# Block products by sevens in the second MLP's up projection, with sums of weights prepared in the first MLP

## The chip, the cores and the metric

The kernel runs on one core of a Trainium2 chip. TensorE multiplies (PE in the profile; PEld is its loading of weights), VectorE (DVE), ScalarE (ACT) and GpSimd (POOL) do everything elementwise, and DMA queues, issued mostly from SyncE (SP), move data between DRAM and the chip's memory. The metric is the device time of one execution in microseconds.

## The reference

One inference step of a two-layer decoder trunk, with 512 prompt tokens and 8 sample tokens (520 columns in all) and a model width of 1024. The part that matters here is the MLP of each layer, which both groups of tokens pass through with the same weights:

```python
def sq_relu_mlp(h, g, w_up, w_down):
    a = jax.nn.relu(rmsnorm(h, g) @ w_up)
    return (a * a) @ w_down
hp = hp + sq_relu_mlp(hp, norm_ffn[l], mlp_up[l], mlp_down[l])
hs = hs + sq_relu_mlp(hs, norm_ffn[l], mlp_up[l], mlp_down[l])
```

The up weights are 1024 x 4096 and the down weights 4096 x 1024, in float32. Ahead of the first MLP is a pooling mixer, between the two MLPs lies the attention of the second layer (with a compressed, a selected and a window branch), and a final RMSNorm follows the second MLP.

## The kernel before

Tokens lie along the free dimension (520 columns, handled as two halves of `NH` = 260), features along the 128 partitions. Every float32 product is made from three products of a rounded type: a weight tile is split into a high part (ACT copies it into the rounded type, L221) and a low part (DVE subtracts, `lo_of`, L201), the data likewise, and high x high, high x low and low x high are added up in PSUM (`gemm`, L237). A weight tile is 128 x 8 x 128, 512 KB. A unit is 8 blocks x 3 products x 2 column halves = 48 matmuls of 260 columns.

Each MLP goes through four quarters of its 4096 hidden features. A quarter has 8 up units, one for each 128 hidden features, and then 8 down units, which add the quarter's contribution to the residual `h`. After an up unit `up_post` applies relu, the norm's factor `rn` and the square, and splits the result into a tile `at` (a ring of eight). In the second MLP the down units of the last quarter are cut into column halves (`last_quarter`), so that the final norm of the first half can run early; they start with `at` tile 0 and come to the last tile at the end.

The order of work is written by `run`. It goes through a list of jobs. Each job has a `pe` part (matmuls), a `prep` (the split of its weights), a `post` list (what follows the matmuls: entry d is written d + 1 jobs later) and loads. These two lines set the order:

```python
due = ahead - sum(k > i for k in with_prep[:done])      # after job i: keep two splits ahead
late.setdefault(i + 1 + d, []).insert(0, f)             # entry d of job i's post, ahead of older ones
```

All `late` entries of a job are written before its matmuls, its splits after them. An engine runs its instructions in the order in which they were written. Weight loads go through SP into a ring of three buffers (`wraw`); a load waits until the low part of the split three tiles earlier has read its buffer. The split parts of a weight tile lie in rings of two (`whi`, `wlo`), and a split waits until the matmuls that use the older tile in its place are done. Products lie in PSUM in a ring of two `mm` tiles of two banks each, and `aux` tiles of one bank.

In the first MLP the list also holds fillers, small products for the compressed branch of the sample group. The tuple `FILLERS` says after which of the 64 units one filler comes; some fillers bring a tiny companion job ahead of them:

```python
FILLERS = (0, 1, 1, 1, 0, 1, 1, 0, 0, 1, 1, 1, 1, 0, 1, 1, 0, 1, 1, 0, 0, 1, 0, 1, 0, 1, 0, 1, 0, 1, 1, 1, 0, 0, 0, 1, 1, 0, 1, 1, 0, 1, 0, 0, 0, 1, 0, 0, 1, 1, 0, 1, 0, 1, 0, 1, 0, 1, 0, 0, 0, 1, 1, 1)
```

A filler splits its own data on ACT and DVE (L473 to L477). POOL is idle in the first MLP. In the second MLP there are no fillers. The pool `wz` holds the split weights of the whole last quarter.

Of the kernel before, what the change touches and what calls it, by code (L numbers as in the profile page):

```python
# [151 lines left out]
def trunk(tc, a, o):  # L152
# [23 lines left out]
    hsave = pool("hd", space=bass.MemoryType.DRAM).tile([P, CT, NT], F32, name="hsave")  # L176
# [23 lines left out]
    def lo_of(out, x, hi):  # L200
        V.tensor_tensor(out, x, hi.bitcast(F32), op=OP.subtract)  # L201
# [127 lines left out]
    def norm_job(emit=lambda: None):  # L329
        box = {}  # L330

        def pe():
            for i in range(2):
                box[i] = st["aux"]()
                TE.matmul(box[i][:, 0:NH], onesm, accn[:, i * NH:(i + 1) * NH], start=True, stop=True)  # L335

        def post():
            inv_rms(box)
            emit()

        return Job(pe=pe, post=post)
# [353 lines left out]
    def mlp_jobs(l, filler, done, before=lambda: None):  # L695
        ap, kind = {}, "w2" if l else "w"

        def open_a():
            ap["p"] = pool("ap")
            if l:  # L700
                pool("wz")
# [21 lines left out]
        js = []  # L723
        for q in range(4):
            for f in range(8):
                js.append(gemm_job(W(a["up"][l, 8 * q + f]), xpairs, up_post(8 * q + f), kind=kind))
                if not l and q in (1, 2):
                    js[-1].after = lambda x=("wink", "winv")[q - 1], b=f: S.dma_start(o[x][b], a_in[x][b])
                if q == f == 0:
                    js[-1].post.insert(0, None)  # L730
                    js[-1].after = lambda: (before(), open_a())
                    js.append(norm_job())
                js += filler()
            for ct in range(CT):
                xs = (lambda q=q: [(at[8 * q + k][:, 0], at[8 * q + k][:, 1]) for k in range(8)])
                if l and q == 3:
                    continue
                js.append(gemm_job(W(a["down"][l, q, ct]), xs, down_post(q, ct), kind=kind))
                js += filler()
        if l:  # L740
            js += last_quarter(xs)
        js.append(Job(hook=lambda: close(*["wz"] * l, "ap")))
        return js

    def last_quarter(xs):


        ws = [W(a["down"][1, 3, ct], home=lambda: (pools["wz"][1], CT)) for ct in range(CT)]
# [24 lines left out]
        def norm(i):  # L773
            sl = slice(i * NH, (i + 1) * NH)
            box = {}

            def pe():
                box["ps"] = st["aux"]()
                TE.matmul(box["ps"][:, 0:NH], onesm, accn[:, sl], start=True, stop=False)  # L779
                TE.matmul(box["ps"][:, 0:NH], onesm, sq[i][:, sl], start=False, stop=True)  # L780

            def post():
                S.activation(rn[:, sl], box["ps"][:, 0:NH], AF.Ln, bias=eps[:, 0:1])  # L783
                S.activation(rn[:, sl], rn[:, sl], AF.Exp, scale=-0.5)  # L784

            def rows(c):
                for ct in (c, c + 1):
                    if i and ct in ahead:
                        G.tensor_tensor(h[:, ct, sl], h[:, ct, sl], rn[:, sl], op=OP.mult)  # L789
                        continue  # L790
                    V.scalar_tensor_tensor(h[:, ct, sl], h[:, ct, sl], gv[:, 5, ct:ct + 1], rn[:, sl], op0=OP.mult, op1=OP.mult)  # L791
                (S if i and c in (2, 6) else nc.sync).dma_start(o["y"][:, c:c + 2, sl], h[:, c:c + 2, sl])
            steps = [lambda c=c: rows(c) for c in range(0, CT, 2)]
            return Job(pe=pe, post=[lambda: (post(), [f() for f in steps])] if i else [post] + steps)

        for i in range(2):
            js += [unit(ct, i) for ct in range(CT)]
        js.insert(CT + 1, norm(0))
        return js + [norm(1)]
# [1151 lines left out]
```

## Time and profile before

| | us |
|---|---|
| median of 3 runs | 1389.52 |
| lowest and highest run | 1387.92, 1392.79 |
| the profiled execution, its time | 1392.16 |
| the profiled execution, its span | 1390.0 |
| TensorE busy in the span | 1345.2 |
| DVE, ACT, POOL busy | 836.7, 570.8, 190.3 |

All further times are those of the one profiled execution, counted from the start of its span. A line of the profile names a line of the kernel (L237), and where a helper writes the instruction, the helper's line. A matmul's own duration is longer than the distance to the next one, because matmuls are pipelined; for the pace, one divides a stretch by its matmuls. The granted clock (PEclk) is TensorE's, as a share of full speed.

### The profile page before, as it was taken

Reading aid. Unit: us, or ns where it says so; the run is one execution under the profiler, and the core shown is the slowest. Engines: PE = TensorE matmul, PEld = TensorE weight load, DVE = VectorE, ACT = ScalarE, POOL = GpSimd, SP = SyncE. Lnnn points to the kernel's source line nnn. Section 1 sums busy time; section 2 is a strip of 40 time slices with the busy share of each in tenths; the row PEclk is TensorE's granted clock in tenths of the full one; section 3 lists DMA queues with packets and bytes.
Section 4 is the critical chain, followed back from the end, with each engine's and each line's share of the span. In section 5 each row is a group of like instructions: output and inputs, shape, how many; then the busy total and the mean of one; then the engine's idle time right before and its main releaser. Section 6 shows DMA issues by size and latency. Waiting matters only on the chain. (4 is left out here: it accounts for less than half of the span.)

```text
span 1390.0 us, 27557 instructions
## 1 busy us (share of the span) xinstructions
PE 1345.2 (97%) x10827; PEld 1261.3 (91%) x10827; DVE 836.7 (60%) x1307; ACT 570.8 (41%) x1012; POOL 190.3 (14%) x265
## 2 busy tenths in 40 slices
PE   7999999999999999999998999998999999999997
PEld 6788999999999999989996777667999999999996
DVE  2788766565565476556878887554554353453563
ACT  3655443333333243464445677563432222221231
POOL 0000000000000000012455764751000000000000
PEclk9999999999999999999999999999999999999999
DMA  7755244554455232339505675766223233322321
GB/s 261 224 153 185 77 136 137 167 165 139 139 172 161 76 107 77 98 131 231 142 26 177 187 207 185 215 204 193 92 87 94 91 94 95 96 92 91 92 91 62
DMA packets 110554, 189.52 MB, mean 136 GB/s; under 512 B 13641, under 2 KB 81482, under 8 KB 109786
## 3 DMA queue, kind: packets, MB, share of 16 engines
q1 hardware_dynamic: 102202, 166.65, 38.6%
q0 software_dynamic: 7168, 12.21, 3.6%
q10 hardware_dynamic: 1056, 8.92, 1.9%
q8 instruction: 85, 1.39, 0.4%
q14 instruction: 43, 0.35, 0.1%
HBM read 177.59 MB, written 16.43 MB: 140 GB/s over the span
## 5 line engine op out<-in xcount | busy, mean ns | idle before, releaser
L237 PE MATMUL mm<-xn,whi 128*128 128x260 f32 (+1 forms) x2784 | 450.0, 284 | 0.4 <-DVE xn L201 0.3
L237 PEld LDWEIGHTS mm<-xn,whi 128*128 128x128 f32 (+1 forms) x2784 | 383.1, 189 | 1.6 <-DVE xn L201 0.5
L201 DVE TENSOR_TENSOR wlo<-wraw,whi 128x1024 fp32r<-128x1024 f32 x163 | 200.6, 1231 | 257.5 <-ACT whi L221 257.2
L237 PE MATMUL mm<-at,whi 128*128 128x260 f32 x2048 | 332.6, 281 | 0.3 <-DVE at L201 0.3
L221 ACT ACTIVATE whi<-wraw 128x1024 fp32r<-128x1024 f32 x163 | 171.5, 1053 | 313.6 <-PE mm L237 257.1
L237 PEld LDWEIGHTS mm<-at,whi 128*128 128x128 f32 x2048 | 283.9, 188 | 1.0 <-DVE at L201 0.5
L237 PE MATMUL mm<-xn,wlo 128*128 128x260 f32 (+1 forms) x1392 | 281.1, 283 | 0.0
L237 PE MATMUL mm<-at,wlo 128*128 128x260 f32 x1024 | 215.9, 282 | 0.0
L237 PEld LDWEIGHTS mm<-xn,wlo 128*128 128x128 f32 (+1 forms) x1392 | 215.2, 188 | 0.0
L237 PEld LDWEIGHTS mm<-at,wlo 128*128 128x128 f32 x1024 | 161.4, 188 | 0.0
L201 DVE TENSOR_TENSOR clo<-craw,chi 128x512 fp32r<-128x512 f32 x128 | 85.3, 686 | 43.6 <-ACT chi L439 28.6
L710 ACT ACTIVATE at<-tmp 128x520 fp32r<-128x520 f32 x64 | 40.9, 639 | 143.2 <-DVE tmp L708 143.2
L1144 POOL TENSOR_TENSOR P<-P,sm 128x1024 f32<-128x1024 f32 (+1 forms) x64 | 81.9, 1290 | 3.8
L711 DVE TENSOR_TENSOR tmp<-tmp 128x520 f32<-128x520 f32 x64 | 44.8, 701 | 45.1 <-ACT at L710 45.1
L1129 ACT ACTIVATE P<-sc,sm 128x512 f32<-128x512 f32 (+3 forms) x128 | 66.0, 529 | 8.4 <-DVE sm L1117 8.2
L818 POOL MEMSET V2c<- 128x1024 f32 x1 | 1.0, 957 | 473.0 <-PE mm L237 473.0
L1244 PE MATMUL pt<-cst,P 128*128 128x128 f32 x320 | 53.0, 282 | 10.5 <-POOL P L1144 5.5
L789 POOL TENSOR_TENSOR h<-h,rn 128x260 f32<-128x260 f32 x2 | 1.9, 946 | 439.7 <-ACT rn L784 439.7
L1244 PEld LDWEIGHTS pt<-cst,P 128*128 128x128 f32 x320 | 37.3, 142 | 26.0 <-issue 6.8
L708 DVE SCALAR_TENSOR_TENSOR tmp<-mm,rn 128x520 f32<-128x520 f32 x64 | 44.5, 695 | 26.1 <-PE mm L237 21.6
L1117 DVE TENSOR_REDUCE sm<-sc 128x2 f32<-128x1024 f32 (+1 forms) x64 | 50.7, 815 | 13.2 <-PE sc L1090 8.8
L439 ACT ACTIVATE chi<-craw 128x512 fp32r<-128x512 f32 x64 | 37.0, 623 | 51.0 <-PE hid L451 35.4
(291 smaller groups left out, 1982.0 us busy)
## 6 DMA issues: line engine op xcount, KB each, us to landing
craw<-in_cc_dram SPq DMA_DIRECT2D x256, 128.0 KB
wraw<-in_up_dram SPq DMA_DIRECT2D x64, 512.0 KB
wraw<-in_down_dram SPq DMA_DIRECT2D x64, 512.0 KB
wraw<-in_selv_dram SPq DMA_DIRECT2D x62, 128.0 KB
wraw<-in_selk_dram SPq DMA_DIRECT2D x59, 128.0 KB
kvs<-in_selk_dram SPq DMA_DIRECT2D x53, 128.0 KB
kvs<-in_selv_dram SPq DMA_DIRECT2D x50, 128.0 KB
wraw<-in_wkv_dram SPq DMA_DIRECT2D x12, 512.0 KB
```

Source lines behind the costliest of these rows:

```text
L201: V.tensor_tensor(out, x, hi.bitcast(F32), op=OP.subtract)
L221: S.activation(hi, raw, AF.Copy)
L237: TE.matmul(ps[0:m, i, 0:NH], wt[:, koff + k, 0:m], x[:, i * NH:(i + 1) * NH], start=(k == 0 and wt is w.hi and x is xh), stop=(k == n - 1 ...
L439: S.activation(hv, src, AF.Copy)
L708: V.scalar_tensor_tensor(halves(r), view(ps), 0.0, halves(rn), op0=OP.max, op1=OP.mult)
L710: S.activation(t[:, 0], r, AF.Square)
L711: V.tensor_mul(r, r, r)
L789: G.tensor_tensor(h[:, ct, sl], h[:, ct, sl], rn[:, sl], op=OP.mult)
L1117: V.tensor_reduce(sm[:, c:c + 2], src, axis=AX.XY if len(src.shape) == 4 else AX.X, op=OP.max, negate=True)
L1129: S.activation(dst, src[:, b], AF.Exp, bias=sm[:, c:c + 1], accum_out=sm[:, m + c:m + c + 1])
L1144: G.tensor_tensor(x, x, sm[:, c:c + 2, None].to_broadcast(list(x.shape)), op=OP.mult)
L1244: TE.transpose(ps[:, 128 * x:128 * x + 128], ab["P", t, s, q][:, c:c + 128], ident)
```

## The change

In quarters 1 to 3 of the second MLP two up units become one pair, and the pair is calculated by Strassen's scheme (in its form with fifteen additions). The 256 x 1024 block of weights and the 1024 x 520 block of data are cut in two in both directions, so that a pair is a product of 2 x 2 blocks; a block of weights is 4 tiles of 128 x 128, a block of data 4 x 128 rows by 260 columns. Seven block products (12 matmuls of 260 columns each) take the place of eight.

- The data's seven left operands `X` are made once, during quarter 0: `normed` scales each tile by norm and weight while the up units run, and `moving` makes the sums and splits them while the down units run. So in these quarters `rn` is already in the data.
- Four of the weights' sums are made during the first MLP: 48 steps (`sum_steps`), each for a quarter of one pair's blocks, load 256 KB by two POOL DMAs, make four additions of 128 x 128 on DVE and store 256 KB by a POOL DMA in `sums` in DRAM. Each buffer exists once. Step n is spread over the `post` of units: a unit's extra entry makes the additions and the store of one step and issues the load of the next.
- A pair loads S13 and S24 (two sums each), A1 (the first tile's weights as they are) and A22 (half a tile). Their split parts go to a ring of four places: the two of `whi` and `wlo`, and two in the memory of `h`'s old tile (`dead`); A22 has its own.
- The seven products run as jobs pe5, pe1, pe6, pe2, pe7, pe3, pe4; the first four carry the splits of S13, A1, S24 and A22, the fifth an empty one. Sums of products are put together on DVE (`common`, `c22`, `c12`, `c21`), relu and squares run on ACT (two squares of each tile), the low part on DVE (`low`). `c22` reads the PSUM bank to which pe4 then adds.
- `open_x` opens the memory for `X` where `wz` was; `wz` is opened after the last pair, with six tiles, and the last quarter's first two weight tiles go to the ring of two.

```diff
-            for f in range(8):
+            if l and q:
+                js += [j for i in range(4) for j in seven_jobs(q, i, at, ap)]
+            for f in range(8 if not (l and q) else 0):
                 js.append(gemm_job(W(a["up"][l, 8 * q + f]), xpairs, up_post(8 * q + f), kind=kind))
...
+        else:
+            steps = [sum_steps(n) for n in range(48)]
+            for j, old, new in zip(units[4:], [()] + steps, [x[:1] for x in steps] + [()]):
+                j.post.append(lambda fs=(*old[1:], *new[:1]): [f() for f in fs])
...
+    def sum_steps(n):
+        pair, j = divmod(n, 4)
+        box = {}
+        def load():
+            box["w"] = pools["pf"][1].tile([P, 2, 2, 128], F32, name="sraw", bufs=1)
+            src = a["up"][1, 8 + 2 * pair:10 + 2 * pair].rearrange("f p (h j) n -> p f h j n", h=2)[:, :, :, j]
+            for f in range(2):
+                G.dma_start(box["w"][:, f], src[:, f])
+        def add():
+            w, x = box["w"], pools["pf"][1].tile([P, 4, 128], F32, name="sout", bufs=1)
+            box["x"] = x
+            V.tensor_tensor(x[:, 0], w[:, 1, 0], w[:, 1, 1], op=OP.add)
+            V.tensor_tensor(x[:, 1], w[:, 0, 0], w[:, 1, 0], op=OP.subtract)
+            V.tensor_tensor(x[:, 2], x[:, 0], w[:, 0, 0], op=OP.subtract)
+            V.tensor_tensor(x[:, 3], w[:, 0, 1], x[:, 2], op=OP.subtract)
+        def store():
+            G.dma_start(sums[pair].rearrange("p (s j) n -> p s j n", j=4)[:, :, j], box["x"])
+        return load, add, store
...
+    def moving(i):
+        x = sv["xt"].rearrange("p (k c) (h n) -> p k h c n", k=2, h=2)
+        B = [[x[:, k, i] for i in range(2)] for k in range(2)]
+        if i == 3:
+            V.tensor_tensor(B[0][0], B[0][1], B[0][0], op=OP.subtract)
...
+        S.activation(sv["X"][:, i, 0], src, AF.Copy)
+        lo_of(sv["X"][:, i, 1], src, sv["X"][:, i, 0])
+    def ring():
+        n = sv["n"]
+        sv["n"] += 1
+        if n % 4 < 2:
+            return [wp.tile([P, 8, 128], F32R, name=x, bufs=2) for x in ("whi", "wlo")]
+        if n == 2:
+            sv["dead"] = con.tile([P, 4, 2, NT], F32R, name="h").rearrange("p t z n -> p t (z n)")
+        return [sv["dead"][:, 2 * (n % 4 - 2) + i, 0:1024].rearrange("p (k n) -> p k n", n=128) for i in range(2)]
+    def seven_jobs(q, i, at, ap):
...
+        S13, A1, S24, A22 = D(s_[:, 0]), D(a["up"][1, f]), D(s_[:, 1]), D(a["up"][1, f + 1][:, 4:8], 4)
+        def times(w, k0, x, out, first=True, last=True):
+            for k in range(4):
+                for wt, part in ((w.hi, 0), (w.hi, 1), (w.lo, 0)):
+                    TE.matmul(out, wt[:, k0 + k], sv["X"][:, x, part, k], start=(first and k == 0 and wt is w.hi and part == 0),
+                              stop=(last and k == 3 and wt is w.lo), skip_group_check=True)
+        def pe7():
+            times(S13, 4, 4, box["e"])
+        def pe4():
+            times(A22, 0, 6, box["e"], first=False)
+        def keep1():
+            box["p1"] = small("p1")
+            S.activation(box["p1"], box["a"], AF.Copy)
+        def common():
+            box["u2"], box["u4"] = small("u2"), small("u4")
+            V.tensor_tensor(box["u2"], box["b"], box["p1"], op=OP.add)
+            V.tensor_tensor(box["u4"], box["c"], box["u2"], op=OP.add)
+        def c22():
+            V.tensor_tensor(box["r"][1][:, NH:], box["e"], box["u4"], op=OP.add)
+        def c12():
+            r = box["r"][0]
+            V.tensor_tensor(r[:, NH:], box["d"], box["u4"], op=OP.add)
+            S.activation(r[:, NH:], r[:, NH:], AF.Relu)
+            squares(0)
+        def c21():
+            r = box["r"][1]
+            V.tensor_tensor(r[:, 0:NH], box["e"], box["u2"], op=OP.add)
+            S.activation(r, r, AF.Relu)
+            squares(1)
...
+        return [job(pe5, S13), job(pe1, A1, keep1), job(pe6, S24, common), job(pe2, A22, c11), nothing(job(pe7, None, c22)),
+                job(pe3, None, c12, lambda: low(0)), job(pe4, None, *((c21, lambda: low(1)) if i < 3 else (lambda: (c21(), low(1)),)))]
```

## Rows read from the trace of the kernel before

**Rows 1.** The page: span, and busy time with share and instructions of TensorE.

```profile
span 1390.0 us, 27557 instructions
...
PE 1345.2 (97%) x10827; PEld 1261.3 (91%) x10827; DVE 836.7 (60%) x1307; ACT 570.8 (41%) x1012; POOL 190.3 (14%) x265
...
```

**Rows 2.** Timeline of the SP queue, two quarters of the second MLP.

```profile
...
1081.32 40.53 SPq L210 DMA_DIRECT2D wraw<-in_up_dram  x8
1127.28 40.49 SPq L210 DMA_DIRECT2D wraw<-in_down_dram  x8
...
```

**Rows 3.** Timeline of ACT: a weight split, second MLP.

```profile
...
1027.28 1.06 ACT L221 ACTIVATE whi<-wraw 128x1024 fp32r<-128x1024 f32 x1 [2.16 <-PE mm L237]
...
```

**Rows 4.** Timeline of DVE around that split.

```profile
...
1028.37 1.23 DVE L201 TENSOR_TENSOR wlo<-wraw,whi 128x1024 fp32r<-128x1024 f32 x1 [1.79 <-ACT whi L221]
1029.51 0.69 DVE L708 SCALAR_TENSOR_TENSOR tmp<-mm,rn 128x520 f32<-128x520 f32 x1
...
```

**Rows 5.** Waits from 1000 us on: us in total, times, longest.

```profile
...
ACT whi L221 <- PE mm L237: 173.4, 53, 4.7
...
```

**Rows 6.** Groups by form, from 960 us on: busy us, mean ns, idle before.

```profile
...
L201 DVE TENSOR_TENSOR wlo<-wraw,whi 128x1024 fp32r<-128x1024 f32 x71 | 87.0, 1225 | 170.3 <-ACT whi L221 170.3
...
L221 ACT ACTIVATE whi<-wraw 128x1024 fp32r<-128x1024 f32 x70 | 74.1, 1059 | 194.3 <-PE mm L237 183.4 <-issue 10.9
L711 DVE TENSOR_TENSOR tmp<-tmp 128x520 f32<-128x520 f32 x32 | 22.4, 700 | 22.6 <-ACT at L710 22.6
...
L710 ACT ACTIVATE at<-tmp 128x520 fp32r<-128x520 f32 x32 | 20.5, 639 | 62.2 <-DVE tmp L708 62.2
...
L760 DVE TENSOR_TENSOR h<-h,mm 128x260 f32<-128x260 f32 x16 | 6.8, 422 | 13.5 <-PE mm L237 13.5
...
L765 ACT ACTIVATE tmp<-h 128x260 f32<-128x260 f32 x14 | 5.9, 422 | 28.1 <-DVE h L760 28.1
...
```

**Rows 7.** Groups by form, whole run: the nearest 128x128 addition.

```profile
...
L1114 DVE TENSOR_TENSOR accn<-sc,sm 128x128 f32<-128x128 f32 x16 | 4.7, 292 | 0.5
...
```

**Rows 8.** Timeline of the SP queue around one weight load.

```profile
...
1092.76 11.77 SPq L210 DMA_DIRECT2D wraw<-in_up_dram  x3
```

**Rows 9.** Windows around that load: busy us, PEclk, DMA share, GB/s.

```profile
...
1093.20:1093.60 0.40, 0.40 (x6) 0.40 (x5) 0.13 (x1) 0.00 (x0) 0.00 (x0) 1.00 0.00 0
1093.60:1094.00 0.40, 0.40 (x5) 0.40 (x5) 0.00 (x0) 0.00 (x0) 0.00 (x0) 1.00 0.53 174
...
1095.60:1096.00 0.40, 0.40 (x6) 0.40 (x5) 0.00 (x0) 0.00 (x0) 0.00 (x0) 1.00 0.05 21
...
```

**Rows 10.** TensorE waits from 100 to 620 us.

```profile
...
PE mm L237 <- DVE xn L201: 0.3, 1, 0.3
```

**Rows 11.** Tile out_kv_dram: POOL issues (ns min/median/max) and landing.

```profile
...
L869 POOL DMA_DIRECT2D out_kv_dram<-kt x12: 542/565/1022, 607.6 to 677.0; - x12
...
DMA to landing us min/median/max: 2.5/3.1/5.3
```

**Rows 12.** Tile Kd: POOL DMA issues and landing.

```profile
...
L891 POOL DMA_DIRECT2D Kd<-Kd x16: 611/627/658, 638.2 to 679.9; - x16
...
DMA to landing us min/median/max: 2.4/5.3/6.6
```

**Rows 13.** Timeline of DVE in the first MLP, two units, a filler between.

```profile
...
339.31 0.70 DVE L718 TENSOR_TENSOR h<-h,mm 128x520 f32<-128x520 f32 x1 [3.58 <-PE mm L237]
340.21 1.23 DVE L201 TENSOR_TENSOR wlo<-wraw,whi 128x1024 fp32r<-128x1024 f32 x1 [0.20 <-ACT whi L221]
...
347.18 0.70 DVE L718 TENSOR_TENSOR h<-h,mm 128x520 f32<-128x520 f32 x1 [1.93 <-PE mm L237]
...
```

**Rows 14.** Chain that ended last, in time, at the last up unit.

```profile
...
1334.00 0.71 DVE at L201
...
1334.76 23.50 PE mm L237 x194
...
```

**Rows 15.** Windows in the attention: busy us of each engine, PEclk, DMA.

```profile
...
730.00:760.00 30.00, 24.80 (x269) 18.49 (x272) 25.62 (x54) 15.02 (x45) 15.52 (x23) 0.90 0.50 170
...
```

More of the change, by code (lines that the diff above doesn't have):

```diff
@@ L175, in trunk @@
     h = con.tile([P, CT, NT], F32, name="h")
-    hsave = pool("hd", space=bass.MemoryType.DRAM).tile([P, CT, NT], F32, name="hsave")
+    hd = pool("hd", space=bass.MemoryType.DRAM)
+    hsave = hd.tile([P, CT, NT], F32, name="hsave")
+    sums = [hd.tile([P, 16, 128], F32, name=f"sums{i}") for i in range(12)]
     ptab = con.tile([1, 2 * DB * NPAGE], I32, name="ptab")
@@ L700, in open_a @@
             if l:
-                pool("wz")
+                open_x()
         at = {}
@@ L731, in mlp_jobs @@
                     js[-1].after = lambda: (before(), open_a())
+                    units.append(js[-1])
                     js.append(norm_job())
+                else:
+                    units.append(js[-1])
+                if l and 1 <= f <= 4:
+                    units[-1].post[0] = lambda x=units[-1].post[0], ct=2 * f - 2: (x(), [normed(c) for c in (ct, ct + 1)])
                 js += filler()
@@ L738, in mlp_jobs @@
                 js.append(gemm_job(W(a["down"][l, q, ct]), xs, down_post(q, ct), kind=kind))
+                units.append(js[-1])
+                if l and not q and ct < 7:
+                    js[-1].post[0] = lambda x=js[-1].post[0], ct=ct: (x(), moving(ct))
                 js += filler()
         if l:
+            js.append(Job(hook=open_z))
             js += last_quarter(xs)
+        else:
+            steps = [sum_steps(n) for n in range(48)]
+            for j, old, new in zip(units[4:], [()] + steps, [x[:1] for x in steps] + [()]):
+                j.post.append(lambda fs=(*old[1:], *new[:1]): [f() for f in fs])
@@ new lines, in ring, with __init__, load, split @@
+    def ring():
[7 more added lines that the diff above has]
+    def seven_jobs(q, i, at, ap):
+        f = 8 * q + 2 * i
+        box = {}
+        class D:
+            def __init__(self, src, n=8):
+                self.src, self.n = src, n
+            def load(self):
+                self.raw = wp.tile([P, 8, 128], F32, name="wraw", bufs=3)
+                nc.sync.dma_start(self.raw[:, 0:self.n], self.src)
+            def split(self):
+                if self.n == 8:
+                    self.hi, self.lo = ring()
+                else:
+                    self.hi, self.lo = (pools["xs"][1].tile([P, 4, 128], F32R, name=x) for x in ("dhi", "dlo"))
+                S.activation(self.hi, self.raw[:, 0:self.n], AF.Copy)
+                lo_of(self.lo, self.raw[:, 0:self.n], self.hi)
+        s_ = sums[4 * (q - 1) + i].rearrange("p (g k) n -> p g k n", g=2)
+        S13, A1, S24, A22 = D(s_[:, 0]), D(a["up"][1, f]), D(s_[:, 1]), D(a["up"][1, f + 1][:, 4:8], 4)
+        def small(name):
+            return pools["xs"][1].tile([P, NH], F32, name=name)
+        def times(w, k0, x, out, first=True, last=True):
[3 more added lines that the diff above has]
+                              stop=(last and k == 3 and wt is w.lo), skip_group_check=True)
+        def pe5():
+            t, u = mm_tile(), None
+            box["c"], box["a"] = t[:, 0, 0:NH], t[:, 1, 0:NH]
+            times(S13, 0, 3, box["c"])
+        def pe1():
+            times(A1, 0, 0, box["a"])
+        def pe6():
+            t = mm_tile()
+            box["b"], box["e"] = t[:, 0, 0:NH], t[:, 1, 0:NH]
+            times(S24, 0, 5, box["b"])
+        def pe2():
+            times(A1, 4, 1, box["a"], first=False)
+        def pe7():
+            times(S13, 4, 4, box["e"])
+        def pe3():
+            box["d"] = st["aux"]()[:, 0:NH]
+            times(S24, 4, 2, box["d"])
+        def pe4():
[7 more added lines that the diff above has]
+            V.tensor_tensor(box["u4"], box["c"], box["u2"], op=OP.add)
+        def c11():
+            box["r"] = [tmp(), tmp()]
+            S.activation(box["r"][0][:, 0:NH], box["a"], AF.Relu)
+        def c22():
[10 more added lines that the diff above has]
+            squares(1)
+        def squares(x):
+            r = box["r"][x]
+            t = at[f + x] = ap["p"].tile([P, 2, NT], F32R, name="at", bufs=8)
+            S.activation(t[:, 0], r, AF.Square)
+            S.activation(r, r, AF.Square)
+        def low(x):
+            lo_of(at[f + x][:, 1], box["r"][x], at[f + x][:, 0])
+        def job(pe, w, *post):
+            return Job(pe=pe, post=list(post), **(dict(loads=[("w2", w.load)], prep=w.split, free_prep={"w2": 1}) if w else {}))
+        def nothing(j):
+            j.prep = lambda: None
+            return j
+        return [job(pe5, S13), job(pe1, A1, keep1), job(pe6, S24, common), job(pe2, A22, c11), nothing(job(pe7, None, c22)),
+                job(pe3, None, c12, lambda: low(0)), job(pe4, None, *((c21, lambda: low(1)) if i < 3 else (lambda: (c21(), low(1)),)))]
@@ L745, in last_quarter @@
     def last_quarter(xs):
-        ws = [W(a["down"][1, 3, ct], home=lambda: (pools["wz"][1], CT)) for ct in range(CT)]
+        ws = [W(a["down"][1, 3, ct], **({} if ct < 2 else dict(home=lambda: (pools["wz"][1], CT - 2)))) for ct in range(CT)]
         js, sq, ahead = [], {}, (3, 5)
```

20 lines of the change are left out of this document (19 added, 1 removed).

## The prediction

> **What bounds the kernel now.** I read the page first: TensorE is busy for 1345 us of a span of 1390 [rows 1], so time is won only by fewer matmuls and lost by every pause of TensorE. Second, the SP queue of the second MLP: eight weight loads for eight up units are followed 45.96 us later by the next eight [rows 2]. Eight units are 384 matmuls, so one takes 45.96 / 384 = 0.1197 us. Third, the timelines of ACT and DVE in one unit. Both run their queue in the order in which it was written. A split of weights on ACT waits for the matmuls that still use its place in the ring of two [rows 3], 53 times in this part of the kernel [rows 5]. DVE then runs the low half of that split and only behind it evacuates a product that was ready before [rows 4]. This is harmless today, because units are 5.74 us long and there is a whole unit of cover; the reader should keep the pattern in mind, since the change cuts the units to a quarter of that length. Fourth, the groups by form give the prices [rows 6, 7].
>
> **What is removed.** 24 up units of 48 matmuls become 12 pairs of 7 x 12: 1152 - 1008 = 144 matmuls, 144 x 0.1197 = 17.2 us. Per pair 1.44 us is saved, and that is the point at which pauses eat the gain: a pair may pause for 1.44 us.
>
> **What is added per pair.** A pair runs its seven products in the order pe5 (S13), pe1 (A1), pe6 (S24), pe2 (A1), pe7 (S13), pe3 (S24), pe4 (A22), each 12 x 0.1197 = 1.44 us, 10.05 us in all. I use 1.06 and 1.23 us for the two halves of a split on ACT and DVE, 0.64 and 0.70 for 520 columns, 0.42 for 260 columns on either [rows 6], and hand-overs of 0.03 between engines; queued neighbours overlap by 0.08 (the evacuation of [rows 4] starts at 1029.51, before the split ends at 1029.60). The sums alone are no alarm: ACT has 3.5 splits, four operations of 260 or 520 columns and four squares, about 8 us, DVE 3.5 splits, five additions and two low halves, about 8 us, of 10.05. What counts is the order.
>
> Pause one, ahead of pe4. pe4 adds onto a bank that c22 reads, so it waits for c22. c22 stands on DVE behind the low half of the next pair's A1, which is written one step earlier, and that split goes to the place in the ring of four which this pair's S13 holds until pe7 ends. From the end of pe7: 0.03 + 1.06 + 0.03 + 1.23 - 0.08 + 0.42 (c22) + 0.03 = 2.72 us, and pe3 covers 1.44: a pause of 1.28.
>
> Pause two, in the next pair's pe6. The split of S24 is written after pe5 of its own pair, so on ACT it stands behind the work of c21, which follows pe4. When pe4 ends, ACT is still busy with c12's relu and squares for 0.59 us (c12 ends on DVE 0.31 us after pe4's start; 0.42 + 2 x 0.64 on ACT with hand-overs last until 2.02, and pe4 until 1.43). Then come relu 0.64, two squares 1.28, the split 1.06 + 1.23 and hand-overs less overlap, 0.04: 4.84 us from the end of pe4 until S24's low half is there. pe5, pe1 and the two matmuls that need only the high half cover 2.87 + 0.24: a pause of 1.73, in two pieces.
>
> Nine pairs have both, 3.01 us. The first pair of a quarter has pause one, and in place of two the A1 split, which waits for the last down unit's place: 0.03 + 1.06 + 0.03 + 1.23 + 0.03 = 2.38, of which pe5 and two matmuls cover 1.68, a pause of 0.7; S24's low half behind it and behind an evacuation comes another 0.3 late. That is 2.3 us. Together 9 x 3.01 + 3 x 2.3 = 34.0 us, net of 17.2: +16.8. The bounds: without the ring's wait pause one is gone (pe3 covers c22) and 1.6 a pair is left, 19 us; without both, nothing. I take the upper value because each term of it is a row of this stage.
>
> The weights' loads grow from 2 to 3.5 tiles a pair. A load is issued at 1092.76 and its traffic runs from 1093.6 to about 1095.6 [rows 8, 9], so it is there after 2.9 us. A1's load can only go once S24's low half has freed its buffer, 4.1 us before ACT can use it: 1.2 us spare, cost nothing; a load over 4.1 us adds its excess nine times.
>
> At the end, the low half of the pair's first tile stands on DVE behind that of its second. The first is wanted after 18 matmuls, 2.15 us, and ready 3.9 us after pe4: a pause of 1.75 where today's is about 0.5 (the low half of [rows 14] ends at 1334.71, the matmul waits until 1334.76): +1.3. The up quarters before it have matmuls for both columns to cover it, 4.3 us.
>
> The first quarter's additions (eight scaled tiles, seven moving blocks and their splits) cost nothing: an up unit holds 1.23 + 3 x 0.70 on DVE and gets two more operations of 0.7, 4.7 of 5.74; a down unit holds 1.9 and gets at most 2.5. Uncovered they would be about 20 us.
>
> **The sums in the first MLP.** There TensorE never waits: one wait of 0.3 us in 520 [rows 10]. 48 steps add four additions each; at 0.29 [rows 7] that is 1.1 us of DVE with overlap. Each step has one buffer, so the chain is: additions end, POOL issues the store (0.55), two loads (0.55 to the second's issue), the second lands, the next additions may start. No load of this kind is in the trace. Nearest is a POOL transfer of 260 KB that lands after 3.1 us, 2.5 to 5.3 [rows 11]; 128 KB within SBUF takes 5.3 in bursts [rows 12]. I take 3.1, because the loads come in twos. The chain from additions to additions is then 0.1 + 0.55 + 0.55 + 3.1 = 4.3, below a unit's 5.74. The Trainium skill (DMA: Bandwidth & Descriptors, Anatomy of one DMA) puts a POOL transfer at 2.0 us plus its bytes at 436 GB/s, an estimate of 2.3 us for 128 KB; by it the loss below would be 14 x 0.8 = 11 us smaller, and no run here shows this load.
>
> But additions are written two jobs behind their unit. Where a unit without a filler is followed by a unit with one, two neighbouring additions are only a filler apart (or a filler's small companion), not a unit. The filler list has 14 such places among the 48. Between the two DVE has about one low half, 1.23, to do, so it stands 4.3 - 1.2 = 3.1 us, and everything behind it stands too: the next split, the filler's splits, an evacuation. With two additions that is 3.1 + 2.1 = 5.2 us late. What DVE has to spare is seen in [rows 13]: it idles 1.93 us before a unit's evacuation where a filler precedes it, 3.58 where none does. Lost per place: 1.6 to 3.3; I take 2.0, since part of it is won back in the next unit: 14 x 2.0 = 28. The bounds are 0 (the spare of two units adds up) and, with 5.3 us landings, 14 x 4.2 = 59.
>
> **Sum.** 1392.2 (the profiled execution) + 16.8 + 1.3 + 28 = 1438.3. It was 2.6 us above the median of the runs, so I predict 1435.7 for a median.
>
> **Rivals.** (1) The sums are hidden: DVE's spare time adds up over two units, as TensorE's silence [rows 10] suggests. Then only the pairs' pauses remain: 1389.5 + 18.1 = 1407.6. Against it: an in-order queue carries one late addition into all that follows. (2) The POOL loads land as in [rows 12], at 5.3: 14 x 2.2 = 31 more, 1466.5. Against: those came three and four at a time. (3) Faster. ACT and DVE stand a job further ahead than I read from the queues, so that the splits of A1 and S24 come before c22 and c21. It decides where a pair pauses for less than 1.44 us, and with nothing left of both pauses, and the sums hidden in the bargain, it gives 1389.5 - 17.2 + 1.3 = 1373.6. For it: neither engine is full. Against: the wait for a place is the longest of ACT's waits [rows 5], and it isn't a matter of being full. (4) TensorE's clock. It was granted 0.90 of full, a mean of its levels of 2.4 and 1.2 GHz, in a stretch where TensorE idled 5.2 of 30 us [rows 15]; a pair would idle 3.0 of 13. At 0.90 the 121 us of matmuls in the pairs lose 12: 1448. The Trainium skill (TensorE: Matmul & The Clock Gate, HAM oscillation) says that idle gaps put the array back to its half clock, which speaks against any change that trades a dense stream for gaps; behind the one pause of 0.5 us 194 matmuls take 23.50 us, 0.121 each [rows 14], no loss of pace; no row shows pauses of 1.6. (5) No change that can be measured: pause two alone, 19 us, against 17.2, and the sums hidden: 1389.5 + 19 - 17.2 + 1.3 = 1392.6.
>
> **Chances.** Forecast 0.55; (1) 0.19; (2) 0.08; (3) 0.07; (4) 0.06; (5) 0.05. A measurement here tells 0.3% (4 us) from no change. So faster 0.07, within 0.3% 0.05, slower 0.88. The range reaches from (1) with pauses a fifth smaller, 1401, to (2), 1466; it leaves out (3), (5) and still slower landings.
>
> **What would show it.** In the profile of the changed kernel: 144 fewer matmuls on TensorE; quarters of up products of about 51.6 us in place of 45.96; pauses of 1.3 ahead of pe4 ended by DVE's c22, and of 1.7 in pe6 ended by the weight split's low half; in the first MLP, TensorE waits that were absent, ended by DVE, while DVE waits for a DMA into the sums' buffer. The prediction is wrong if pairs take under 11.5 us, if the granted clock drops in the pairs, or if the first MLP shows no wait of DVE on a DMA, which makes it 1407.6.

## The result, and the profile after

The change makes the kernel slower: 1491.11 us as the median of 4 runs (1487.2 to 1493.62) against 1390.53, a ratio of 1.0721 (95% interval 1.0686 to 1.0757). The forecast had the sign, 1435.7 us, but not the size; its range ended at 1466. The profiled execution has a span of 1491.8 us, 101.8 more than that of before.

The page of the kernel after, to be read beside [rows 1]: 144 matmuls fewer, as forecast, but TensorE's share falls from 97% to 92%.

```profile
span 1491.8 us, 27973 instructions
...
PE 1365.0 (92%) x10683; PEld 1266.1 (85%) x10683; DVE 907.8 (61%) x1554; ACT 630.3 (42%) x1115; POOL 288.9 (19%) x409
```

Lines have moved: L239 is now the matmul of `gemm`, L203 `lo_of`, L862 the matmul of a pair's products, L850 the high half of a pair's split, L496 a filler's product (`hid`).

The SP queue's timeline, which answers to [rows 2], says where the time went: each row is the start of a quarter's down loads in the second MLP. First the row of before that the first of them is compared with, then those after:

```profile
1035.43 40.49 SPq L210 DMA_DIRECT2D wraw<-in_down_dram  x8
```

```profile
1098.33 40.49 SPq L212 DMA_DIRECT2D wraw<-in_down_dram  x8
1205.76 36.52 SPq L212 DMA_DIRECT2D wraw<-in_down_dram  x8
1309.40 36.86 SPq L212 DMA_DIRECT2D wraw<-in_down_dram  x8
1414.84 29.74 SPq L212 DMA_DIRECT2D wraw<-in_down_dram  x8
```

So 62.9 us were lost by then and 101.8 - 62.9 = 38.9 behind it. Up to that row the change touches the first MLP and, in the second, the scaling of the data; the run without the sums, below, shows that the second costs nothing there. The quarter from 1205.76 to 1309.40 takes 103.64; the one that ended at 1127.28 in [rows 2] took 1127.28 - 1035.43 = 91.85.

**The first MLP.** The same 400 us in both kernels, first before, then after (window, its length, TensorE's busy time and matmuls, the granted clock, DMA share, GB/s):

```profile
200.00:600.00 400.00, 399.92 (x3327) 1.00 0.41 129
```

```profile
200.00:600.00 400.00, 360.62 (x2817) 0.94 0.57 176
```

There are 510 matmuls fewer in 400 us, at 400 / 3327 = 0.1202 each 61.3 us. TensorE idles 39.4 us of it. The other 21.9 passed while matmuls ran slower: nine stretches at a granted clock of 0.50, 37 us together, account for about 18 of them. Who made TensorE and DVE wait, in the views of waits from 200 to 600 us (total, times, longest); before, TensorE's list held 0.3 us [rows 10]:

```profile
PE mm L239 <- DVE wlo L203: 20.9, 7, 7.2
PE hid L496 <- DVE clo L203: 15.5, 5, 4.8
...
DVE sout L782 <- DMA sraw<-in_up_dram: 88.6, 26, 5.0
```

The timeline of DVE around the longest of these waits:

```profile
314.99 0.29 DVE L785 TENSOR_TENSOR sout<-sraw,sout 128x128 f32<-128x128 f32 x1
...
323.52 0.29 DVE L782 TENSOR_TENSOR sout<-sraw 128x128 f32<-128x128 f32 x1 [4.36 <-DMA sraw<-in_up_dram]
...
324.25 0.29 DVE L785 TENSOR_TENSOR sout<-sraw,sout 128x128 f32<-128x128 f32 x1
...
329.10 0.29 DVE L782 TENSOR_TENSOR sout<-sraw 128x128 f32<-128x128 f32 x1 [4.22 <-DMA sraw<-in_up_dram]
...
330.04 1.22 DVE L203 TENSOR_TENSOR wlo<-wraw,whi 128x1024 fp32r<-128x1024 f32 x1
```

And that of TensorE, with the windows behind it:

```profile
331.31 0.80 PE L239 MATMUL mm<-xn,wlo 128*128 128x260 f32 x2 [7.23 <-DVE wlo L203]
```

```profile
331.31:335.35 4.04, 4.04 (x19) 4.04 (x19) 3.12 (x6) 0.74 (x2) 1.16 (x2) 0.50 0.79 257
335.35:339.00 3.65, 3.65 (x33) 3.65 (x32) 2.87 (x4) 1.59 (x2) 0.00 (x0) 1.00 0.50 152
```

DVE stands twice behind a load that has not landed, 4.36 and 4.22 us; a weight's low half stands behind the second, and TensorE gets it 7.23 us late. Then 19 matmuls run at a granted clock of 0.50, the lower of its two levels (1.2 of 2.4 GHz), in 4.04 us: 0.21 each, where the next window, at 1.00, has 3.65 / 33 = 0.11 (a window also counts the matmuls that lie across its edges).

**The pairs.** TensorE's waits from 1060 us on:

```profile
PE mm L862 <- DVE u L898: 14.1, 12, 1.5
PE mm L862 <- DVE tmp L905: 12.3, 12, 1.2
PE mm L862 <- DVE wlo L203: 6.1, 9, 0.8
PE mm L862 <- ACT whi L850: 3.6, 6, 0.6
PE mm L862 <- DVE h L203: 2.3, 3, 0.8
PE mm L862 <- ACT h L850: 1.8, 3, 0.6
PE mm L239 <- DVE at L203: 1.6, 1, 1.6
```

The second row is the forecast's pause one, rows three to six are pause two in its two pieces, the last is the wait at the end. The first row is a third pause that the forecast lacks. One pair on TensorE's timeline (pe6's start, its low half, pe2, pe4), and DVE around it:

```profile
1181.69 0.50 PE L862 MATMUL mm<-X,whi 128*128 128x260 f32 x2 [0.59 <-ACT whi L850]
1182.95 0.39 PE L862 MATMUL mm<-X,wlo 128*128 128x260 f32 x1 [0.76 <-DVE wlo L203]
...
1185.57 0.48 PE L862 MATMUL mm<-X,whi 128*128 128x260 f32 x2 [1.14 <-DVE u L898]
...
1191.31 0.51 PE L862 MATMUL mm<-X,dhi 128*128 128x260 f32 x2 [1.18 <-DVE tmp L905]
```

```profile
1184.53 0.43 DVE L897 TENSOR_TENSOR u<-mm,p 128x260 f32<-128x260 f32 x1 [0.42 <-PE mm L862]
1184.99 0.43 DVE L898 TENSOR_TENSOR u<-mm,u 128x260 f32<-128x260 f32 x1
...
1189.69 1.23 DVE L203 TENSOR_TENSOR h<-wraw,h 128x1024 fp32r<-128x1024 f32 x1 [3.14 <-ACT h L850]
1190.83 0.42 DVE L905 TENSOR_TENSOR tmp<-mm,u 128x260 f32<-128x260 f32 x1
```

pe2 adds onto a and starts at 1185.57, when `common` has read c for u4, though pe2 does not touch c: c and a are the two banks of one tile. pe4 starts when c22 (L905) is through, which stood behind the next split's low half, as forecast. A quarter's 720 matmuls are 86.2 us at 0.1197; 103.64 - 86.2 = 17.5 in four pairs is 4.4 us idle per pair, where the forecast had 3.0. It is about 0.75 + 1.02 for pause two, 1.31 for the third and 1.34 for pause one, each from the end of the matmuls in front to the next start.

### The profile page after: what moved, and what is told of

It is laid out like the page before. It is cut to its first block, busy times and chain, and to the rows that moved or that the text cites. A ratio compares the mean times of both kernels' runs of the same rounds, so it can differ in the third digit from the quotient of the medians.

```text
span 1491.8 us, 27973 instructions
## 1 busy us (share of the span) xinstructions
PE 1365.0 (92%) x10683; PEld 1266.1 (85%) x10683; DVE 907.8 (61%) x1554; ACT 630.3 (42%) x1115; POOL 288.9 (19%) x409
## 5 line engine op out<-in xcount | busy, mean ns | idle before, releaser
L239 PE MATMUL mm<-at,whi 128*128 128x260 f32 x2048 | 332.9, 282 | 1.6 <-DVE at L203 1.6
L239 PE MATMUL mm<-xn,whi 128*128 128x260 f32 (+1 forms) x2016 | 332.4, 288 | 1.0 <-ACT whi L223 0.7
L203 DVE TENSOR_TENSOR wlo<-wraw,whi 128x1024 fp32r<-128x1024 f32 x157 | 193.0, 1230 | 204.0 <-ACT whi L223 167.8
L239 PEld LDWEIGHTS mm<-xn,whi 128*128 128x128 f32 (+1 forms) x2016 | 284.2, 193 | 2.5 <-ACT whi L223 0.9
L239 PEld LDWEIGHTS mm<-at,whi 128*128 128x128 f32 x2048 | 284.2, 188 | 2.2 <-DVE at L203 1.8
L223 ACT ACTIVATE whi<-wraw 128x1024 fp32r<-128x1024 f32 x139 | 145.7, 1050 | 211.1 <-PE mm L239 136.3
L239 PE MATMUL mm<-xn,wlo 128*128 128x260 f32 (+1 forms) x1008 | 207.7, 288 | 15.4 <-DVE wlo L203 15.4
L239 PE MATMUL mm<-at,wlo 128*128 128x260 f32 x1024 | 216.0, 282 | 5.5 <-DVE wlo L203 5.5
L239 PEld LDWEIGHTS mm<-xn,wlo 128*128 128x128 f32 (+1 forms) x1008 | 159.1, 192 | 16.6 <-DVE wlo L203 16.5
L239 PEld LDWEIGHTS mm<-at,wlo 128*128 128x128 f32 x1024 | 161.5, 188 | 5.9 <-DVE wlo L203 5.9
L203 DVE TENSOR_TENSOR clo<-craw,chi 128x512 fp32r<-128x512 f32 x128 | 85.3, 686 | 34.3 <-ACT chi L441 25.1
L788 POOL DMA_DIRECT2D sums<-sout x48 | 35.0, 729 | 354.4 <-DVE sout L785 334.7
L479 ACT ACTIVATE dhi<-tmp 128x512 fp32r<-128x512 f32 x32 | 20.2, 632 | 161.2 <-DVE tmp L477 157.3
L777 POOL DMA_DIRECT2D sraw<-in_up_dram x96 | 67.7, 712 | 26.2 <-DMA wraw<-in_up_dram 25.4
L782 DVE TENSOR_TENSOR sout<-sraw 128x128 f32<-128x128 f32 x48 | 13.8, 288 | 88.6 <-DMA sraw<-in_up_dram 88.6
L712 ACT ACTIVATE at<-tmp 128x520 fp32r<-128x520 f32 x40 | 25.6, 639 | 90.1 <-DVE tmp L710 90.1
L862 PE MATMUL mm<-X,h 128*128 128x260 f32 x360 | 51.3, 293 | 11.3 <-DVE u L898 7.2
```

What stands on the lines that cost most here:

```text
L223: S.activation(hi, raw, AF.Copy)
L239: TE.matmul(ps[0:m, i, 0:NH], wt[:, koff + k, 0:m], x[:, i * NH:(i + 1) * NH], start=(k == 0 and wt is w.hi and x is xh), stop=(k == n - 1 ...
L479: S.activation(y[0], d, AF.Copy)
L777: G.dma_start(box["w"][:, f], src[:, f])
L788: G.dma_start(sums[pair].rearrange("p (s j) n -> p s j n", j=4)[:, :, j], box["x"])
L862: TE.matmul(out, wt[:, k0 + k], sv["X"][:, x, part, k], start=(first and k == 0 and wt is w.hi and part == 0), stop=(last and k == 3 and w ...
```

## The experiments

In what follows "the second MLP's part" is the stretch from its first down load to the end of the profiled span: 354.6 us before, 393.5 after.

**The sums left out.** The pairs load plain weights.

```diff
-            steps = [sum_steps(n) for n in range(48)]
...
-        S13, A1, S24, A22 = D(s_[:, 0]), D(a["up"][1, f]), D(s_[:, 1]), ...
+        S13, A1, S24, A22 = D(a["up"][1, f]), D(a["up"][1, f]), D(a["up"][1, f + 1]), ...
```

> Left out: the weights' sums are not made; the pairs load plain up weights of the same size in their place. Theory: of the 101 us lost, 63 came before the second MLP's first down load (so the first MLP, where the sums are made) and 39 behind it, so this runs at 1390.5 + 39 = 1430 us (1424 to 1436), the first MLP without a pause and at a granted clock of 1.00 as before. The forecast's own sizes (sums 28, pairs and end 18) give 1408.6. Rival: the loss in the first MLP comes from something else of the change, then it stays and the time is near 1491.

Measured: 1432.94 us, as the theory has it. The first down load starts at 1035.29, and TensorE has no wait above 0.3 in the first MLP. The second MLP's part is 395.6.

**The sums alone.** The pairs, their moving blocks and tiles are taken out.

```diff
-            if l and q:
-                js += [j for i in range(4) for j in seven_jobs(q, i, at, ap)]
-            for f in range(8 if not (l and q) else 0):
+            for f in range(8):
```

> Left out: the pairs; all up products are as before and the sums are made but not used. Theory: the first MLP alone costs 63, so 1390.5 + 63 = 1453 us (1447 to 1459). By the forecast's size for the sums, 28, it would be 1419. Rival: part of the 63 is only an early start of the pairs' weight loads or other work that the pairs bring; then it is clearly below 1447.

Measured: 1455.51 us, first down load at 1098.24, where it stood at 1098.33 after the change; the second MLP's part is 355.8, near that of before. So each half of the loss comes with its own part of the change. (By the medians the two runs lose 42.8 and 65.3 us, 7.5 more together than the 100.6 of the change; the first MLP's loss alone differs by up to 9 between executions of the same instructions.)

**The additions left out.** POOL stores what it loaded.

```diff
         def add():
+            return
...
-            G.dma_start(sums[pair]..., box["x"])
+            G.dma_start(sums[pair]..., box["w"].rearrange("p f h n -> p (f h) n"))
```

> Left out: the four additions of each step; what was loaded is stored as it is, so the 96 loads and 48 stores of POOL and their bytes stay, and DVE has no part in the steps. Theory (DVE, in order, stands behind a load that has not landed, and all of its queue is late): the first MLP's loss goes, 1491 - 63 = 1428 us (1422 to 1436), no wait of TensorE there above 1 us. Rival, the added DRAM traffic (12.6 MB in, 12.6 MB out) delays the weights: the loss stays, 1480 or more. Rival, DVE is too full by the additions' own 1.1 us a step: also about 1428, told apart by the run that keeps the additions on DVE and loads earlier.

Measured: 1427.39 us, first down load at 1034.85. All of the added traffic is there and costs TensorE nothing.

**The additions on POOL.**

```diff
-            V.tensor_tensor(x[:, 0], w[:, 1, 0], w[:, 1, 1], op=OP.add)
+            G.tensor_tensor(x[:, 0], w[:, 1, 0], w[:, 1, 1], op=OP.add)
```

and the other three likewise.

> The four additions of a step run on POOL instead of DVE, nothing else. Theory: POOL stands behind the loads and nothing of the first MLP is queued behind POOL that TensorE wants soon: 1428 us (1422 to 1436). Rival, traffic: 1480 or more. Rival, POOL falls behind by its slower additions (a step is then about 0.7 + 1.4 + 4.3 of store, loads and landing and 4 x 0.4 of additions, 8.0 us against a mean distance of steps of about 8.3): then later work on POOL, or the first pair's load of its sums, waits, 1440 or more.

Measured: 1430.86 us. The window from 200 to 600 us is that of before again; the groups by line show that POOL now does the waiting, and an addition costs it over twice what it cost DVE:

```profile
200.00:600.00 400.00, 399.92 (x3327) 1.00 0.59 182
```

```profile
L785 POOL TENSOR_TENSOR sout<-sraw,sout 128x128 f32<-128x128 f32 x41 | 27.7, 675 | 3.2
L782 POOL TENSOR_TENSOR sout<-sraw 128x128 f32<-128x128 f32 x40 | 25.5, 637 | 141.4 <-DMA sraw<-in_up_dram 141.4
```

**Two buffers, additions on DVE.**

```diff
-            box["w"] = pools["pf"][1].tile([P, 2, 2, 128], F32, name="sraw", bufs=1)
+            box["w"] = pools["pf"][1].tile([P, 2, 2, 128], F32, name="sraw", bufs=2)
...
-            w, x = box["w"], pools["pf"][1].tile([P, 4, 128], F32, name="sout", bufs=1)
+            w = box["w"]
+            V.tensor_tensor(w[:, 1, 1], w[:, 1, 0], w[:, 1, 1], op=OP.add)
...
-                j.post.append(lambda fs=(*old[1:], *new[:1]): [f() for f in fs])
+                j.post.append(lambda fs=(*new[:1], *old[1:]): [f() for f in fs])
```

> The additions stay on DVE, four a step, but are made in place, and the space of the second buffer becomes a second buffer for the loads, so that a step's load is issued a step earlier (the order of the blocks in DRAM and in the products follows). Theory (DVE stands behind landings): two additions close together find the second's data landed or 1 us short of it, and the first MLP loses 0 to 17 of its 63: 1428 to 1445 us, DVE's waits on the sums' loads under 25 us in all. Rival, DVE is too full by the additions themselves: the waits of TensorE stay, 1475 or more.

Measured: 1447.39 us, 2 above the theory's range; first down load at 1051.83, so 16.4 of the 62.9 are left. DVE still makes all additions, and its waits on the loads fall from 88.6 us in 26 to this:

```profile
DVE sraw L781 <- DMA sraw<-in_up_dram: 20.2, 9, 3.7
```

**a in a tile of its own.**

```diff
-            box["c"], box["a"] = t[:, 0, 0:NH], t[:, 1, 0:NH]
+            box["c"], box["a"] = t[:, 0, 0:NH], st["aux"]()[:, 0:NH]
```

> Only a, the sum of pe1 and pe2, moves: from the second bank of the tile that holds c to a tile of its own. Theory of the pause that the forecast lacks: pe2 adds onto a, and what orders it counts the whole tile, so it waits until DVE has read c for u4, two additions behind pe6; without that, 1.31 us in each of 12 pairs go: 1491 - 15.7 = 1475 us (1471 to 1479), no wait of TensorE on u. Rival: the pause moves to a product behind it (pe4, which waits for the same u4 through c22) and the time stays at 1488 or more.

Measured: 1481.31 us, 9.8 less, where 15.7 were expected: between theory and rival. The second MLP's part is 380.6, 12.9 less. The wait on u is gone from the list:

```profile
PE mm L862 <- DVE tmp L905: 18.8, 12, 2.5
PE mm L862 <- DVE wlo L203: 4.4, 6, 0.8
```

In nine pairs the gain is there. In the first pair of a quarter pe4 now waits up to 2.48 us: the split of the next A1 stands on ACT behind its load, and c22 behind that split.

```profile
1165.78 1.06 ACT L850 ACTIVATE whi<-wraw 128x1024 fp32r<-128x1024 f32 x1 [2.25 <-DMA wraw<-in_up_dram]
```

**S24's split two steps earlier.** Each pair's jobs pe3, pe4 and the next pe5 carry the splits of the next pair's S13, A1 and S24.

```diff
...
+              job(pe3, n13, c12, lambda: low(0)), job(pe4, n1, ...)]      # n13, n1, n24: of the next pair
+        own = (S13, A1, S24) if i == 0 else (sv.pop("s24"), None, None)
```

> Only the split of the next pair's S24 moves: it is written two steps earlier, ahead of c12's and c21's work on ACT. Theory (pause two, in pe6, comes from S24's split behind c21's relu and squares): 1.77 us in each of 9 pairs go: 1491 - 16 = 1475 us (1470 to 1480). Rival: the split then delays c12 and c21, so that their low halves or the next pair's p1 are late instead: 1485 or more.

Measured: 1468.77 us. The second MLP's part is 375.2, 18.3 less; pause two's rows are gone but for three waits of about 0.5 in first pairs. The clock stays at 1.00 in all its windows of 50 us from 1100 to 1450, so some 3 of the 18.3 us are clock (compare the windows after the change at the next run). (The first MLP, the same in both, was 6.2 us shorter in this profile.)

**c22 ahead of A1's low half.** pe3 carries an empty split as well, so that those behind it are written a step later.

```diff
-                job(pe3, None, c12, lambda: low(0)), job(pe4, ...
+                nothing(job(pe3, None, c12, lambda: low(0))) if i < 3 else job(pe3, ...), job(pe4, ...
```

> Only the splits of the next pair's S13 and A1 move: each is written a step later, so that c22 stands on DVE behind the low half of S13 (whose place is long free) and ahead of that of A1, in the 9 pairs that have a next one in their quarter. Theory (pause one, ahead of pe4): 1.34 shrinks to about 0.3 in 9 pairs: 1491 - 9.4 = 1482 us (1478 to 1486). Rival: the pause comes from c22's own chain from pe7 (0.5 us behind it) and the places of the splits do nothing: 1489 or more.

Measured: 1499.57 us, 8.5 slower than the change. Neither theory: pause one is gone in all nine pairs, and the waits ahead of pe6 grow, since c12 on DVE, and so c21's work and S24's split on ACT, come later.

```profile
PE mm L862 <- ACT whi L850: 9.0, 6, 1.5
PE mm L862 <- DVE wlo L203: 6.1, 9, 0.8
PE mm L862 <- ACT h L850: 4.2, 3, 1.5
PE mm L862 <- DVE tmp L905: 3.6, 3, 1.2
```

Summed, TensorE's waits are even 1.3 us less than after the change. But the granted clock now falls once in each quarter of pairs, where 1.5 and 0.8 us lie close together in one product. After the change it stays at 1.00 in the first two of these quarters and falls in the third, at the same pauses. First this run, then the last windows after the change:

```profile
1200.00:1250.00 50.00, 44.28 (x342) 0.93 0.35 110
1250.00:1300.00 50.00, 44.62 (x359) 1.00 0.35 113
1300.00:1350.00 50.00, 42.10 (x319) 0.93 0.36 110
1350.00:1400.00 50.00, 44.76 (x362) 1.00 0.35 112
1400.00:1450.00 50.00, 40.40 (x299) 0.93 0.41 125
```

```profile
1350.00:1400.00 50.00, 44.49 (x344) 0.97 0.36 111
1400.00:1450.00 50.00, 40.64 (x306) 0.97 0.36 121
```

Three windows at 0.93 are 3 x 50 x 0.07 = 10.5 us of pace, against 3 for the two at 0.97. That is the likely reason why the run is slower with shorter waits; no run separates it, and in the profiled executions the second MLP's part is only 3.1 us longer than after the change (396.6).

**All three orders.** a and e in tiles of their own, pe7 ahead of pe2, c22 ahead of A1's split, S24's split early.

```diff
...
+        js = [job(pe5, own[0]), job(pe1, own[1], keep1), job(pe6, own[2], common), job(pe7, A22, c22), job(pe2, None, c11),
+              job(pe3, n13, c12, lambda: low(0)), job(pe4, n1, ...)]
...
```

> All three pauses at once: a and e have tiles of their own, pe7 runs ahead of pe2 (so that S13's place comes free a product earlier), c22 is written ahead of the split of the next pair's A1, and S24's split ahead of c12's and c21's work. The sums stay as in the change. Theory (the three pauses come from the order of the queues and from whole-tile waits, not from the amount of work): a pair takes 10.1 to 10.6 us in place of 14.5, except the first of each quarter, and 9 to 12 pairs win 4.0: 1491 - 36 to 48 = 1443 to 1455. Rival, ACT and DVE are too full at 8 us of a 10 us pair, as the run with only c22 moved hints, where the pause ahead of pe4 came back ahead of pe6: the pairs stay above 12 us and the time above 1465.

Measured: 1450.43 us; the second MLP's part is 354.3, 39.2 less, which is all that it had lost (38.9). A later quarter takes 90.8 us, a pair 10.05 + (90.8 - 86.2) / 4 = 11.2, more than the 10.1 to 10.6 expected.

**The orders, with the additions on POOL.** The last edit together with `G.tensor_tensor` for the four additions:

```diff
-            V.tensor_tensor(x[:, 0], w[:, 1, 0], w[:, 1, 1], op=OP.add)
+            G.tensor_tensor(x[:, 0], w[:, 1, 0], w[:, 1, 1], op=OP.add)
```

> The orders of the run with all three pauses removed, and the additions of the sums on POOL. Theory (the losses of the two places add up, and the saved 144 matmuls, 17.2 us, then remain): 1390.5 - 17.2 plus what the first pairs of the quarters and the end still lose, 3 to 12: 1376 to 1386, faster than before by 0.3 to 1%. Rival, the saving is eaten by a rest of pauses and by the clock: 1390 or more.

Measured: 1390.23 us, ratio 0.9999 (0.9986 to 1.0012): no change, above what the theory gave; the rival was right. The second MLP's part is 352.4, only 2.2 of the saved 17.2 us less than before. TensorE's waits there are 11.8 us, where before they were 0.8. The largest is pe2's, for p1:

```profile
PE aux L868 <- ACT p L899: 7.0, 9, 1.2
```

**c21 two steps later, A22's split one earlier,** on top of that.

```diff
-        job(pe4, n1, *((c21, lambda: low(1)) if i < 3 else ...
+        job(pe4, n1, *((None, None, c21, lambda: low(1)) if i < 3 else ...
...
-        job(pe6, own[2], common), job(pe7, A22, c22)
+        job(pe6, A22 if i else S24, common), job(pe7, None if i else A22, c22)
```

> On top of the run with the new orders and the additions on POOL: c21 with its relu and squares is written two steps later (behind p1 of the next pair) and the split of A22 one step earlier, in pairs that have a next one. Theory: what is left in the pairs is pe2's wait for p1, which stands on ACT behind c21's three operations and A22's split, 7.0 us in 9 pairs plus some 0.2 each of restart; S24's load, which waits for the buffer that A22's split frees, also goes earlier. So 9 us less, 1390.2 - 9 = 1381 us (1377 to 1384), faster than before by 0.4 to 0.9%. Rival: ACT is full (8.9 of 10 us), c21's work then delays the splits of the next pair and the time stays at 1388 or more.

Measured: 1389.0 us, ratio 0.9989 (0.9974 to 1.0004). The wait for p1 went and came back ahead of pe4, as a wait on c22; the rival was right:

```profile
PE e L868 <- DVE tmp L911: 6.2, 9, 1.9
```

ACT and DVE have about 8 us each in a pair of 10 (7.7 and 7.4 us busy in a pair after the change), and this shift alone only moved the pause.

**Less work on ACT, and another place for the first pair.**

```diff
-            S.activation(r, r, AF.Square)
+            if i < 3:
+                G.tensor_tensor(r, r, r, op=OP.mult)
...
-        if n % 4 < 2:
+        if n % 4 in (0, 2):
```

> The orders and the additions on POOL of the run before the last, with four edits more: A22's split a step earlier; c21 one step later; in pairs that have a next one the second square (r times r) of both tiles on POOL instead of ACT, their low halves written later; and the first pair's A1 split goes to a place that is long free, S24's to the place of the last down unit. Theory: ACT has 1.3 us less in each of 9 pairs, so that p1 and c22 are no longer late (0.3 to 1.1 a pair), and the first pairs lose the waits of pe1 and pe4 (0.6 and 1.4 to 1.9): 12 to 8 us less than 1390, 1378 to 1382, 0.5 to 0.9% under the time of before. Rival: POOL's squares (about 1.9 us each by the 0.95 us for 260 columns) make the low halves late for DVE, and the pauses return in another place: 1388 or more.

Measured: 1382.43 us, just above the theory's range; ratio 0.9931 (0.9914 to 0.9949): 0.7% faster than the kernel before, with an interval clear of 1. A later quarter takes 87.0 us, where before it took 91.85:

```profile
1135.17 31.22 SPq L212 DMA_DIRECT2D wraw<-in_down_dram  x8
1222.14 31.22 SPq L212 DMA_DIRECT2D wraw<-in_down_dram  x8
```

Of the second MLP's 354.6 us 345.3 are left, 9.3 less. The four new edits were not tried one by one, so how much each gives is not shown.

## Why the prediction was too low

**Saved matmuls: right.** 144, and with the pauses nearly gone the last run shows most of the saving: 4.9 us in a later quarter, where 48 matmuls are 5.7.

**The sums in the first MLP: right mechanism, mis-sized term.** "The chain from additions to additions is then 0.1 + 0.55 + 0.55 + 3.1 = 4.3, below a unit's 5.74" is the step that failed. For the sums' loads the profile after has:

```profile
L777 POOL DMA_DIRECT2D sraw<-in_up_dram x96: 707/714/729, 134.9 to 578.7; - x96
...
DMA to landing us min/median/max: 2.7/4.3/7.3
```

The price was taken from [rows 11], issue 0.565 and landing 3.1; here an issue takes 0.71 and the landing 4.3 in the median (2.7 to 7.3), between [rows 11] and [rows 12], 5.3. With the median the chain is 0.30 to the store's issue, 0.65 and 0.71 of issues and 4.3, together 6.0: longer than a unit.

DVE's timeline above has a short and a long chain. Additions that end at 324.54 are followed by the next at 329.10, 4.56 later, close to the forecast's 4.3. Those that end at 315.28 are followed by the next at 323.52, 8.24 later, though a unit lies between. So DVE waits 26 times, not 14. By the order of its queue 14 of these waits are at the places that the forecast counted, 4.1 us each for its 3.1: in nine of the 14 the chain is 4.4 to 4.8, as forecast, but in eight of these only about 0.3 us of DVE's work lies between the additions, where the forecast set off a low half of 1.2; in the other five it is 6.0 to 8.8. The other 12, 2.6 us each, come behind at least one whole unit, where the forecast had no wait at all. At TensorE the 26 waits cost 39.4 / 26 = 1.5 us of idling each, less than the forecast's 2.0 a place; the count and, below, the clock make the difference. Rival (2) had a long landing, 5.3, but still the 14 places. Why the landing differs so much was not tried.

The Trainium skill (DMA: Bandwidth & Descriptors, Anatomy of one DMA), by which the landing was an estimate of 2.3 us, lies lower still; the trace disagrees with it here, 2.7 at the least.

**The clock: rival (4), in another place.** The forecast gave it 0.06 and placed it in the pairs. It fell in the first MLP, at a price of about 18 of the 21.9 us, nearly half of what the waits themselves cost. In the pairs it fell only in the third quarter. The Trainium skill (TensorE: Matmul & The Clock Gate, HAM oscillation) says that idle gaps put the array back to its half clock, and the trace agrees: 0.50 behind the 7.23 us wait, though 1.00 behind one of 3.58. Summed, 39.4 + 21.9 = 61.3 of the 62.9; the forecast's 28 had neither the count nor the clock.

**Rival (1), sums hidden:** false, shown by the run of the sums alone (65 us). Two other causes are out: the traffic costs nothing (the run without additions), and DVE has room for the additions (the run with two buffers keeps them and wins 46 of 63 us).

**Pause one: right,** 1.34 measured for 1.28, and its cause is shown: it went when c22 was written ahead of A1's low half.

**Pause two: right,** 1.77 for 1.73, and shown: 18.3 us with S24's split earlier, 16 expected, and the rest is near the 3 us of clock.

**The third pause: missing.** The forecast has no term for it, since it looked for the readers of the bank that a product writes to. What orders pe2 also counts the reader of the other bank of its tile. The run with a in a tile of its own, in which the wait is gone, shows it. 12 x 1.31 = 15.7 of the 20.8 us by which the second MLP's loss, 38.9, is above the forecast's 18.1. Near 4 us more are clock: from 1350 on three windows of 50, 50 and 42 us have 0.97, 0.97 and 0.92, 6.4 us of pace, where before the last 25 us at 0.90 cost 2.5. What lowered it there was not tried.

**Loads at no cost: right for the change, not behind it.** As soon as a pause is gone, the next wait in a quarter's first pair is for A1's load (2.25 us). **The end: right,** 1.6 us waited for the low half where the list of before has 0.3: +1.3, as forecast.

**Rival (3), splits far enough ahead:** false for this order, but the last run, with splits and sums moved out of TensorE's way, comes to within 9 us of its time (1373.6).

Open: why the first MLP's loss differs by up to 9 us between executions of the same instructions (first down loads at 1089.6 to 1099.1), and a part of the saving in the last run: of 17.2 us it shows 9.3, its waits in the second MLP are 5.1 us longer than before (5.9 for 0.8), and 2.8 stay unexplained.

## What to carry to other kernels

An in-order engine that everyone waits for should not stand behind a DMA: give the step that waits to an engine nobody waits for (POOL here, at twice the price per addition and no cost), or load a step earlier. Cutting units to a quarter of their length uses up the cover that made the order of the queues harmless, so each split and evacuation must be placed anew; a pause that is removed by reordering alone can come back elsewhere. Here it went when work was also taken off ACT, though that edit was not tried by itself. When two accumulators share a tile, look for the readers of both.

## What the runs showed of the hardware

Waits cost more than their length: behind nine of the twelve waits of 0.9 us and more in the first MLP the granted clock was 0.50 for about 3 to 6 us. It was not the length alone: a wait of 3.58 us, like ones of 1.89 and 1.00, was followed by 1.00, one of 2.49 by 0.50 within 2 us. In the pairs after the change, four pauses of 0.6 to 1.2 us in a pair of 14.5 left the clock at 1.00 in four windows of 50 us, but in the third quarter the same pauses came with 0.97 in two windows. With one product's two pauses lengthened to 1.5 and 0.8 it fell to 0.93 in one window of each quarter. So the lengths of the pauses alone do not tell when it falls.

A 128x128 addition took 0.60 to 0.68 us on POOL and 0.28 on DVE, a 128x520 product 1.05 on POOL and a square of that size 0.64 on ACT. With the additions on POOL, the sums' three DMAs a step raised the traffic from 129 to 182 GB/s between 200 and 600 us, and TensorE's busy time there stayed at 399.92.
